# Row maxima of 32 x 512 x 1024 floats on one core: a new choice of the rows that GpSimd takes from VectorE

**Chip, cores, metric.** One core of a Trainium2 chip. The metric is the device time of one execution in microseconds (us). The span of a profile is shorter than that time, by 1.7 to 1.9 us for nearly all kernels here; two kernels that are an exception matter below.

## The reference

```python
x = np.random.randn(32, 512, 1024).astype(np.float32)   # 67.1 MB
def reference(x):
    return np.max(x, axis=-1)
```

The kernel must read all of x once. In the profile of the kernel before, the queue that does it is busy 96.7% of the span of 162.3 us, and its last piece lands at 158.98 us.

## The kernel before

The 16384 rows lie on 128 partitions. A load brings n rows to every partition ("row" is from here on a row on each of the 128 partitions, thus 128 x 1024 numbers). Loads 0 to 16 bring 15, 15, 15, 14, 12, 11, 9, 8, 7, 6, 4, 3, 2, 2, 1, 1 and 1 rows into a ring, and three pieces bring the last two rows. One queue on SyncE issues them all.

VectorE reduces rows along the free dimension. To spare it work in the late part, some 128-column parts of some late loads go another way: TensorE turns them (128 x 128 transposes into PSUM), ScalarE copies them to SBUF, GpSimd takes the maximum over the partitions, TensorE brings the one row of result back into a column, and VectorE merges. `SHARED` says which: load: (rows, parts of eight).

```python
SHARED = {7: (2, 3), 9: (4, 4), 11: (3, 3), 13: (2, 3), 16: (1, 1)}
TENSOR = [("turn", 7, 0), ("back", 7, 0), ("turn", 9, 0), ...]   # order on TensorE
MERGE = {8: (7,), 12: (9,), 15: (11,), 18: (13, 16)}             # behind which load to merge
...
    # turn(j, c): q rows by `parts` transposes, then
    in_turn("ACT", nc.scalar.copy(out=sb[:, :W], in_=ps[:, :W]))
    in_turn("POOL", nc.gpsimd.partition_all_reduce(
        top[:, :W], sb[:, :W], P, bass_isa.ReduceOp.max))
...
    # for each load j on VectorE:
        if n > m:
            maximum(res[:, col:col + n - m], rows(j)[:, :n - m, :])        # whole rows
        if m and parts < C:
            maximum(share(j)[:, parts, :], rows(j)[:, n - m:, parts * P:]) # the rest of shared rows
        merge(j)
...
    # the end: three pieces with the last two rows
    latest_row = maximum(res[:, AT - 1:AT], piece)          # piece 1: 689 columns
    merge(len(loads))
    maximum(<two results>, <piece 2 and what piece 1 gave>) # the pair, 2 x 336 columns
    merge(len(loads) + 1)
    maximum(res[:, I - 1:I], res[:, MID - 1:])              # piece 3: 689 columns
    # stores: three behind latest_row, the last behind everything
```

A row that is shared with all eight parts needs no partial reduction on VectorE; a row with three parts needs one of 640 columns.

## Time and profile before

| | before |
|---|---|
| median time | 164.06 us (163.99 to 164.13, 6 runs) |
| span of the profile | 162.3 us |
| DMA queue of the loads | 96.7% of the span |
| VectorE (DVE) busy | 135.4 us, 83% |
| GpSimd busy | 16.2 us |

The chain of work that ended last, by engine, and the group of GpSimd's all-reduces (busy us, mean ns of one, and idle time before them):

```profile
DVE 57%; DMA 36%; issue 5%; DVEq 0%
...
L143 POOL PARTITION_ALL_REDUCE top<-sb x7 | 16.0, 2330 | 141.8 <-ACT sb L141 141.8
```

The chain names VectorE as the main limit.

### The profile page before, as it was taken

What the parts mean: (1) busy time and instruction counts of PE and PEld (TensorE: products, weight loads), DVE (VectorE), ACT (ScalarE), POOL (GpSimd) and SP (SyncE); (2) the same over time, 40 slices, a digit from 0 to 9 for tenths busy, and PEclk for the clock granted to TensorE, in tenths of its full rate; (3) what the DMA queues carried; (4) which work ended last, traced back from release to release, by engine and by line L of the source; (5) the groups of instructions that cost most, each with busy time, mean ns of one, the idle gap of its engine ahead of it and who ended that gap; (6) DMA issues with size and microseconds to landing.
All of it is one profiled execution on the core that took longest, in us unless ns stands there. A gap on an engine that the chain in (4) does not pass through costs nothing.

```text
span 162.3 us, 305 instructions
## 1 busy us (share of the span) xinstructions
PE 14.0 (9%) x76; PEld 12.0 (7%) x76; DVE 135.4 (83%) x35; ACT 6.3 (4%) x8; POOL 16.2 (10%) x11
## 2 busy tenths in 40 slices
PE   0000000000000000000000000000003010736540
PEld 0000000000000000000000000000002010725440
DVE  3000079995999779998999999999999999999994
ACT  3000000000000000000000000000001000222020
POOL 0000000000000000000000000000000500095970
DMA  7999699988999699999998998999999999999990
GB/s 242 485 485 454 273 485 485 485 379 348 485 485 485 285 410 452 452 452 388 497 472 371 433 455 355 436 436 420 509 396 445 452 395 396 440 411 423 405 379 18
DMA packets 3200, 67.18 MB, mean 414 GB/s; under 512 B 640, under 2 KB 640, under 8 KB 1408
## 3 DMA queue, kind: packets, MB, share of 16 engines
q1 hardware_dynamic: 2880, 67.11, 96.7%
q10 hardware_dynamic: 320, 0.07, 0.2%
HBM read 67.11 MB, written 0.07 MB: 414 GB/s over the span
## 4 chain that ended last, share of the span: by engine, by line
DVE 57%; DMA 36%; issue 5%; DVEq 0%
DVE res L168 52%; DMA ring<-in_x_dram 36%; DVE fetched L168 5%; DVEq L249 0%
## 5 line engine op out<-in xcount | busy, mean ns | idle before, releaser
L168 DVE TENSOR_REDUCE res<-ring 128x15 f32<-128x15360 f32 (+10 forms) x15 | 124.1, 8302 | 23.7 <-DMA ring<-in_x_dram 23.7
L143 POOL PARTITION_ALL_REDUCE top<-sb x7 | 16.0, 2330 | 141.8 <-ACT sb L141 141.8
L135 PE MATMUL ps<-ident,ring 128*128 128x128 f32 x38 | 9.3, 425 | 133.8 <-DMA ring<-in_x_dram 133.8
L135 PEld LDWEIGHTS ps<-ident,ring 128*128 128x128 f32 x38 | 7.5, 223 | 134.1 <-issue 127.8
L141 ACT COPY sb<-ps 128x768 f32<-128x768 f32 (+3 forms) x7 | 5.1, 739 | 150.2 <-PE ps L135 150.2
L168 DVE TENSOR_REDUCE fetched<-ring 128x2 f32<-128x1280 f32 (+3 forms) x5 | 8.5, 1699 | 0.0
L161 PE MATMUL fetched<-ident,top 1*128 1x1 f32 x38 | 4.8, 243 | 10.8 <-DVE fetched L168 7.3
L161 PEld LDWEIGHTS fetched<-ident,top 1*128 1x128 f32 x38 | 4.5, 213 | 12.5 <-issue 8.0
L168 DVE TENSOR_REDUCE res<-res 128x2 f32<-128x672 f32 (+1 forms) x2 | 1.7, 858 | 0.0
L141 ACT ACT_TABLE_LOAD x1 | 1.3, 1283 | 0.7 <-PEq L238 0.7
L83 DVE MEMSET ident<- 128x128 f32 x1 | 0.2, 165 | 0.8 <-PEq L238 0.8
L168 DVE TENSOR_REDUCE res<-fetched 128x2 f32<-128x8 f32 (+3 forms) x5 | 0.7, 158 | 0.0
L90 DVE TENSOR_SCALAR rowno<-rowno 32x1 f32<-32x1 f32 x3 | 0.4, 146 | 0.1
L85 DVE TENSOR_TENSOR_SCAN colno<-ident 128x128 f32<-128x128 f32 x1 | 0.4, 425 | 0.0
L92 DVE TENSOR_SCALAR ident<-colno,rowno 128x128 f32<-128x128 f32 x1 | 0.3, 285 | 0.0
L87 DVE STREAM_TRANSPOSE rowno<-colno 128x32 f32<-128x32 f32 x1 | 0.2, 213 | 0.0
L238 POOL MEMSET const-float32-0.0<- 128x1 f32 x1 | 0.1, 98 | 0.2 <-issue 0.2
L238 POOL MEMSET const-bfloat16-1.0<- 128x1 bf16 x1 | 0.1, 101 | 0.0
L238 POOL MEMSET const-uint8-127<- 128x1 uint8 x1 | 0.1, 101 | 0.0
L238 POOL MEMSET const-float32-1.0<- 128x1 f32 x1 | 0.1, 99 | 0.0
L84 DVE MEMSET rowno<- 128x32 f32 x1 | 0.1, 85 | 0.0
## 6 DMA issues: line engine op xcount, KB each, us to landing
ring<-in_x_dram SPq DMA_DIRECT2D x3, 7680.0 KB, 38.4
ring<-in_x_dram SPq DMA_DIRECT2D x1, 7168.0 KB, 37.0
ring<-in_x_dram SPq DMA_DIRECT2D x1, 6144.0 KB, 33.4
ring<-in_x_dram SPq DMA_DIRECT2D x1, 5632.0 KB, 28.6
ring<-in_x_dram SPq DMA_DIRECT2D x1, 4608.0 KB, 39.1
ring<-in_x_dram SPq DMA_DIRECT2D x1, 4096.0 KB, 33.3
ring<-in_x_dram SPq DMA_DIRECT2D x1, 3584.0 KB, 29.0
ring<-in_x_dram SPq DMA_DIRECT2D x1, 3072.0 KB, 35.9
```

The source lines that it names most:

```text
L83: in_turn("DVE", nc.vector.memset(ident, 1.0))
L84: in_turn("DVE", nc.vector.memset(rowno, 0.0))
L85: in_turn("DVE", nc.vector.tensor_tensor_scan(out=colno, data0=ident, data1=ident, initial=-1.0, op0=ALU.add, op1=ALU.mult))
L87: in_turn("DVE", nc.vector.transpose(out=rowno, in_=colno[:, :32]))
L90: in_turn("DVE", nc.vector.tensor_scalar(out=part, in0=part, scalar1=float(q * 32), scalar2=None, op0=ALU.add))
L92: in_turn("DVE", nc.vector.tensor_scalar(out=ident, in0=colno, scalar1=rowno[:, 0:1], scalar2=None, op0=ALU.is_equal))
L135: in_turn("PE", nc.tensor.transpose(out=ps[:, k * P:(k + 1) * P], in_=rows(j)[:, loads[j][1] - m + r + i, c0 * P:(c0 + 1) * P], identity=i ...
L141: in_turn("ACT", nc.scalar.copy(out=sb[:, :W], in_=ps[:, :W]))
L143: in_turn("POOL", nc.gpsimd.partition_all_reduce(top[:, :W], sb[:, :W], P, bass_isa.ReduceOp.max))
L161: in_turn("PE", nc.tensor.transpose(out=share(j)[:, c0, r + i:r + i + 1], in_=tops[j, c][0:1, k * P:(k + 1) * P], identity=ident[0:1, 0:1],))
L168: return in_turn("DVE", nc.vector.reduce_max(out=out, in_=in_, axis=X))
L238: nc = _bacc.Bacc("TRN2", target_bir_lowering=False, num_devices=1)
```

## The change

The intent: give GpSimd a different set of parts. One full row each of loads 8, 10 and 11 (all eight parts, so no partial reduction is left for VectorE), and three parts of three rows of load 9 and of two rows of load 13. Loads 7 and 16 are no longer shared. 38 parts become 39, seven all-reduces become six. The load sizes do not change. Line numbers in the changed kernel are one lower.

```diff
-SHARED = {7: (2, 3), 9: (4, 4), 11: (3, 3), 13: (2, 3), 16: (1, 1)}
+SHARED = {8: (1, 8), 9: (3, 3), 10: (1, 8), 11: (1, 8), 13: (2, 3)}
 TENSOR = [
-    ("turn", 7, 0), ("back", 7, 0), ("turn", 9, 0), ("turn", 9, 1),
-    ("back", 9, 0), ("turn", 11, 0), ("turn", 11, 1), ("back", 9, 1),
-    ("turn", 13, 0), ("back", 11, 0), ("back", 11, 1), ("turn", 16, 0),
-    ("back", 13, 0), ("back", 16, 0),
+    ("turn", 8, 0), ("back", 8, 0), ("turn", 9, 0), ("turn", 9, 1),
+    ("turn", 10, 0), ("back", 9, 0), ("back", 9, 1), ("turn", 11, 0),
+    ("back", 10, 0), ("turn", 13, 0), ("back", 11, 0), ("back", 13, 0),
 ]
-MERGE = {8: (7,), 12: (9,), 15: (11,), 18: (13, 16)}
+MERGE = {9: (8,), 10: (9,), 12: (10,), 15: (11,), 18: (13,)}
```

## The prediction

> **What bounds the kernel now.** I read the page first: busy shares, groups, chain. Here is its page, in pieces.
>
> ```profile
> span 162.3 us, 305 instructions
> ...
> PE 14.0 (9%) x76; PEld 12.0 (7%) x76; DVE 135.4 (83%) x35; ACT 6.3 (4%) x8; POOL 16.2 (10%) x11
> ...
> q1 hardware_dynamic: 2880, 67.11, 96.7%
> ...
> L168 DVE TENSOR_REDUCE res<-ring 128x15 f32<-128x15360 f32 (+10 forms) x15 | 124.1, 8302 | 23.7 <-DMA ring<-in_x_dram 23.7
> L168 DVE TENSOR_REDUCE fetched<-ring 128x2 f32<-128x1280 f32 (+3 forms) x5 | 8.5, 1699 | 0.0
> ```
>
> Two things are nearly full: the 16 DMA engines (96.7%) and VectorE (DVE), whose only real idle time is 23.7 us, all spent waiting for a load. The early timeline puts that idle time before 74.64 us (18.91 + 1.98 + 1.99 + 0.79 us before the first four loads, 0 to 3), so DVE works without a visible gap from 74.64 us to its last reduction. That looks DVE-bound, in which case every column taken off DVE would pay. So the next question is how late the loads land. A landing is the issue time from the timeline of the load queue plus the time to landing from the DMA issues in the same narrow window; for loads 10, 12 and 16 and for the last piece:
>
> ```profile
> 103.47 0.42 SPq L185 DMA_DIRECT2D ring<-in_x_dram  x1
> ring<-in_x_dram SPq DMA_DIRECT2D x1, 2048.0 KB, 40.3
> 114.78 0.43 SPq L185 DMA_DIRECT2D ring<-in_x_dram  x1
> ring<-in_x_dram SPq DMA_DIRECT2D x1, 1024.0 KB, 35.2
> 131.63 0.33 SPq L185 DMA_DIRECT2D ring<-in_x_dram  x1
> ring<-in_x_dram SPq DMA_DIRECT2D x1, 512.0 KB, 24.7
> 147.52 0.33 SPq L207 DMA_DIRECT2D res<-in_x_dram  x1
> res<-in_x_dram SPq DMA_DIRECT2D x1, 344.0 KB, 11.5
> ```
>
> That gives 143.8, 150.0, 156.3 and 159.0 us. In the same way, from the records themselves to a hundredth: load 7 lands at 123.10, 8 at 131.62, 9 at 138.92, 10 at 143.81, 11 at 147.50, 12 at 149.98, 13 at 152.47, 14 at 153.76, 15 at 155.04, 16 at 156.31, the three pieces at 157.22, 158.13 and 158.98. DVE's timeline of the last stretch:
>
> ```profile
> 143.83 4.42 DVE L168 TENSOR_REDUCE res<-ring 128x4 f32<-128x4096 f32 x1
> ...
> 155.06 1.22 DVE L168 TENSOR_REDUCE res<-ring 128x1 f32<-128x1024 f32 x1
> ...
> 156.34 1.09 DVE L168 TENSOR_REDUCE fetched<-ring 128x1 f32<-128x896 f32 x1
> ...
> 157.34 0.86 DVE L168 TENSOR_REDUCE res<-ring 128x1 f32<-128x689 f32 x1
> ...
> 158.24 0.85 DVE L168 TENSOR_REDUCE res<-res 128x2 f32<-128x672 f32 x1
> 159.01 0.22 DVE L168 TENSOR_REDUCE res<-fetched 128x2 f32<-128x8 f32 x2
> 159.15 0.86 DVE L168 TENSOR_REDUCE res<-res 128x1 f32<-128x689 f32 x1
> ```
>
> DVE starts each load's work within a few hundredths to some tenths of its landing: load 10 after 0.02 us, 15 after 0.02, 16 after 0.03, the last piece after 0.17. So DVE's continuity hides a tie: from about 140 us on, DVE and the loads arrive together, and whatever DVE saves early it spends waiting. Only what DVE does after 156.31 us can move the end.
>
> [...] 15 rows take 16154 ns and one row 1214 ns, thus 1067 ns a row and 147 ns fixed, of which some 85 ns lie under the next instruction (starts 143.83 and 148.17 are 4.34 us apart, the duration is 4.42). [...] 2048 columns took 2.27 us (from 139.41) beside a GpSimd that was idle, and 2.28 us (from 141.60 and from 150.23) beside its all-reduce. [...] the windows show 442 GB/s at 20 to 40 us and 414 to 428 between 139 and 151 us. [...]
>
> **The change part by part.** A "part" is 128 columns of a row. Taken from DVE before: 2x3 + 4x4 + 3x3 + 2x3 + 1 = 38 parts; after: 8 + 3x3 + 8 + 8 + 2x3 = 39. One part is 1067 / 8 = 133 ns of DVE.
>
> *Instructions on DVE.* Of the reductions of rows straight into the result, loads 11 and 16 get one each again (13 alone has none): 15 become 17. Of the partial reductions into fetched, only those of loads 9 and 13 stay: 5 become 2. The merges stay five. So DVE has one instruction less, some 60 ns of unhidden fixed cost, and 133 ns less work: in all about 0.2 us less busy time of 135.4.
>
> *Loads.* The sizes do not change. Every slot that a late load reuses belonged to loads 0 to 5, and the last issues waited for landings eight loads before (131.63, 138.93, 143.82 and 147.52 us follow the landings of loads 8 to 11). Nothing that the change moves releases a load; the landings should stay where they are.
>
> *DVE replayed against the landings*, with durations from the groups by shape and about 0.085 us overlap: load 7 starts at 123.96 as now, eight whole rows give 8.59, so load 8 starts at 132.55 (0.74 later than now). Its six rows: 6.46, to 139.01. Load 9: three rows 3.26, partial 2.06, merge 0.08: to 144.41, where now load 10 starts at 143.83. Load 10 with three rows instead of four: 3.26, merge 0.08: 147.75 (now 148.17). Load 11 with two rows: 2.19: 149.94. Load 12 has landed only at 149.98, so it starts at 150.0, 2.19 and a merge 0.09: 152.28, where load 13 has landed only at 152.47. So the 0.25 us by which DVE now comes to load 12 after its landing is gone, and what DVE saved is spent in two waits (about 0.05 and 0.2 us). From load 13 on the sequence is as now: 152.49, 153.88, 155.06, 156.20 for the merge of load 11.
>
> *The end.* Load 16 starts at 156.34 as now, but reads 1024 columns in place of 896: 1.21 us in place of 1.09, +0.12. Its own merge (start to start 0.07) is gone, with the transpose, copy and all-reduce of that row. The last reduction thus starts at 159.15 + 0.12 - 0.07 = 159.20, and the last store goes out 0.05 us later. Sum: +0.05 us on 164.05.
>
> *GpSimd's chain.* All-reduces by width: 1024 columns 3.2 us, 768 2.5, 384 1.5. After: 1024, 768, 384, 1024, 1024, 768, together 16.1, in place of the 16.0 busy us of seven calls. Load 8: lands 131.62, transposes 1.9, copy 1.0, all-reduce 3.2: to 138.0, eight transposes back by 139.1, needed at 144.3. Load 9: all-reduces end at 144.0 and 145.5; its transposes back stand behind load 10's turn on TensorE (to 145.8) and are done by about 147.0, needed at 147.67. Load 10: copy done 146.9, all-reduce to 150.2, back by 151.3, needed at 152.2. Load 11: all-reduce 150.7 to 153.9, back by about 155.0, needed at 156.2. Load 13: 155.0 to 157.5, back by 158.3, needed at 159.1. Each has at least 0.6 us to spare by this estimate.
>
> **The rivals.** *A, DVE-bound:* the lack of idle time before every late reduction speaks for it. Then the 0.2 us saved would arrive at the end: 163.85. Against it stand the landings: the last piece lands at 158.98 and its reduction already starts at 159.15, so no more than 0.17 can come off, and in the replay DVE meets landings at load 12 to 16 first. *B, the merge of load 9 or 11 is late:* GpSimd now hands back three whole rows, and load 9's merge comes one load after its own instead of three. If its transposes back ended 1 us later than I place them, DVE would stand 0.3 to 0.5 us there; load 12's wait of 0.05 and load 13's of 0.2 would swallow half: 164.2 to 164.4. It needs an all-reduce that takes longer than its width says; the two 1024-column ones took 3.22 and 3.30, so I give it little. *C, the landings move* because fewer or other readers touch the ring: [...] a shift of a few tenths either way remains. *D, a whole-row share is cheap enough to be a real gain over 2%,* 3.3 us: DMA busy 96.7% of the span leaves no room.
>
> **Range and chances.** My path gives 164.1, A 163.85, B up to 164.4; the spread of the runs before is 0.08 us. So the predicted time is 164.1 us, the range 163.8 to 164.4. A 2% difference needs 3.3 us, which none of these reaches: faster 0.01, same 0.98, slower 0.01.
>
> **What would show it.** In the changed profile: landings within 0.1 us of those above; DVE busy about 135.2 us; gaps before the reductions of loads 12 and 13 of 0.05 and 0.2 us, in which the releaser is a load; six all-reduces in place of seven; load 8's work starting near 132.55, load 16's at 156.34 with 1.21 us, the last reduction near 159.2. I am wrong if DVE waits for TensorE or fetched before a merge (rival B), if load 16's work starts earlier than 156.3 us (the landings moved), or if the last reduction starts before 159.1 us with the landings in place (rival A).

The forecast's sum is +0.12 - 0.07 = +0.05 us on 164.05 us.

## The result and the profile after

The changed kernel took 164.18 us in the median (164.00 to 164.21, 6 runs) against 164.06 us: ratio 1.0006, 95% interval 0.9993 to 1.0019. It is the same at 2%, and inside the predicted range. Ratios here are the mean time of one kernel's fast runs over the mean of the other's of the same rounds, so they are not quite the ratios of the medians.

The page of the changed kernel, with the lines that answer to those above:

```profile
span 162.4 us, 298 instructions
...
PE 14.2 (9%) x78; PEld 12.1 (7%) x78; DVE 135.3 (83%) x34; ACT 6.3 (4%) x7; POOL 16.3 (10%) x10
...
q1 hardware_dynamic: 2880, 67.11, 96.6%
...
DMA 58%; DVE 39%; SPq 0%; issue 0%; DVEq 0%
...
L167 DVE TENSOR_REDUCE res<-ring 128x15 f32<-128x15360 f32 (+10 forms) x17 | 128.4, 7593 | 23.7 <-DMA ring<-in_x_dram 23.7
L142 POOL PARTITION_ALL_REDUCE top<-sb x6 | 16.1, 2697 | 141.1 <-ACT sb L140 141.1
...
L167 DVE TENSOR_REDUCE fetched<-ring 128x3 f32<-128x1920 f32 (+1 forms) x2 | 3.6, 1824 | 0.2 <-DMA ring<-in_x_dram 0.2
```

The counts are those of the diff: 17 reductions from the ring straight into the result (the first piece's among them), 2 partial ones, 6 all-reduces. The chain has turned from "DVE 57%, DMA 36%" to "DMA 58%, DVE 39%", though neither the loads nor VectorE's total work has changed by more than some tenths of a us. The reason is the last line: VectorE now idles visibly for 0.2 us before a partial reduction, waiting for a load, and a chain that is followed back from the end switches to DMA at that gap. Before, VectorE met the loads with no gap, so the chain stayed on VectorE. Here VectorE and the loads run level, and a gap of 0.2 us was enough to turn the shares.

VectorE's timeline of the last stretch in the changed kernel (start, duration, both in us):

```profile
150.00 2.29 DVE L167 TENSOR_REDUCE res<-ring 128x2 f32<-128x2048 f32 x1
152.20 0.16 DVE L167 TENSOR_REDUCE res<-fetched 128x1 f32<-128x8 f32 x1
152.56 1.50 DVE L167 TENSOR_REDUCE fetched<-ring 128x2 f32<-128x1280 f32 x1 [0.20 <-DMA ring<-in_x_dram]
...
156.34 1.22 DVE L167 TENSOR_REDUCE res<-ring 128x1 f32<-128x1024 f32 x1
...
158.37 0.85 DVE L167 TENSOR_REDUCE res<-res 128x2 f32<-128x672 f32 x1
159.14 0.16 DVE L167 TENSOR_REDUCE res<-fetched 128x2 f32<-128x8 f32 x1
159.26 0.87 DVE L167 TENSOR_REDUCE res<-res 128x1 f32<-128x689 f32 x1
```

The landings of loads 7 to 16 and of the pieces differ from those before by at most 0.02 us (load 16: 156.31 in both; last piece: 158.98 in both). VectorE arrives early at load 12 and load 13 and waits; load 16's work starts at 156.34 as before; from there on the path is 0.11 us longer (the last reduction starts at 159.26 in place of 159.15).

### The profile page after: what moved, and what is told of

The parts are those of the page before. It is cut to its first block, busy times and chain, and to the rows that moved or that the text cites. A ratio compares the mean times of both kernels' runs of the same rounds, so it can differ in the third digit from the quotient of the medians.

```text
span 162.4 us, 298 instructions
## 1 busy us (share of the span) xinstructions
PE 14.2 (9%) x78; PEld 12.1 (7%) x78; DVE 135.3 (83%) x34; ACT 6.3 (4%) x7; POOL 16.3 (10%) x10
## 4 chain that ended last, share of the span: by engine, by line
DMA 58%; DVE 39%; SPq 0%; issue 0%; DVEq 0%
DMA ring<-in_x_dram 58%; DVE res L167 38%; DVE fetched L167 1%; SPq L184 0%; DVEq L167 0%
## 5 line engine op out<-in xcount | busy, mean ns | idle before, releaser
L167 DVE TENSOR_REDUCE res<-ring 128x15 f32<-128x15360 f32 (+10 forms) x17 | 128.4, 7593 | 23.7 <-DMA ring<-in_x_dram 23.7
L140 ACT COPY sb<-ps 128x1024 f32<-128x1024 f32 (+2 forms) x6 | 5.0, 852 | 148.0 <-PE ps L134 148.0
L167 DVE TENSOR_REDUCE fetched<-ring 128x3 f32<-128x1920 f32 (+1 forms) x2 | 3.6, 1824 | 0.2 <-DMA ring<-in_x_dram 0.2
L167 DVE TENSOR_REDUCE res<-fetched 128x1 f32<-128x8 f32 (+2 forms) x5 | 0.8, 157 | 0.0
```

What stands on the lines that cost most here:

```text
L167: return in_turn("DVE", nc.vector.reduce_max(out=out, in_=in_, axis=X))
```

## The experiments

Theory: **the landing of load 16 and VectorE's work after it set the end; work saved before it turns into waiting.** Rival A: VectorE is the bound from 74.64 us on and each column counts. Rival B: a merge waits for GpSimd's way. Rival C: landings depend on VectorE or on who reads the ring.

A yardstick is needed, since single runs of one kernel differ by some tenths of a us (the changed kernel by 0.6 us in its second set). The records of the profiled executions show one cause: the first load lands somewhat earlier or later (21.23 to 21.53 us), and all later landings move along with it; from load 0's landing to load 16's it took 134.90 to 134.97 us in every profile. So I compare the time from load 16's landing to the start of the last reduction, the **tail**, as well as mean times.

| run | load 16 lands | last reduction starts | tail | mean time, and of the kernel before in the same rounds |
|---|---|---|---|---|
| kernel before | 156.31 | 159.15 | 2.84 | |
| changed kernel | 156.31 | 159.26 | 2.95 | 164.16, 164.06 |
| changed, again | 156.17 | 159.12 | 2.95 | 164.26, 164.03 |
| load 16 shared again | 156.28 | 159.18 | 2.90 | 164.14, 164.03 |
| before, load 16 whole | 156.33 | 159.27 | 2.94 | 164.19, 164.03 |
| load 16: two parts shared | 156.38 | 159.33 | 2.95 | 164.32, 164.03 |
| load 11's merge late | 156.15 | 159.12 | 2.97 | 164.15, 164.08 |
| half the columns | 156.24 | 159.18 | 2.94 | 164.22, 163.97 |
| load 8 cut | 156.35 | 159.29 | 2.94 | 164.18, 164.02 |
| dummy behind load 12 | 156.34 | 159.28 | 2.94 | 164.26, 164.08 |
| dummy behind load 16 | 156.31 | 159.45 | 3.14 | 164.35, 164.08 |
| load 9 back late | 156.31 | 161.77 | 5.46 | 166.68, 163.97 |
| second row of load 8 | 156.46 | 159.40 | 2.94 | 164.87, 164.08 |
| 16 idle transposes | 156.36 | 159.31 | 2.95 | 164.91, 164.02 |

Landings and the last starts are from each trace's records. A tail comes from one profile, and of the kernel before only one is kept; but eight of the profiles (the changed kernel twice and six of its or the old kernel's variants) have the same work on VectorE behind load 16, and their tails agree within 0.01 us. In time, every run is "the same" as the kernel before at 2%. The 95% interval of the ratio lies wholly above 1 only for "two parts shared", "dummy behind load 16", "load 9 back late" and the last two rows; differences of 0.1 us between the others are told by the tail, not by the time.

### 1. The changed kernel again

> The changed kernel once more, as the base for the runs beside it. My theory (the landing of load 16 at 156.31 us and what VectorE does after it set the end): last reduction starts at 159.26 us as before in its profile, time some 0.1 us over the kernel before, 164.15 to 164.2. Rival A (VectorE is the bound from 74.64 us on, every column counts): 0.2 us under the kernel before.

Tail 2.95 us again; ratio 1.0013 (interval 1.0000 to 1.0026). The changed kernel is if anything slower by 0.1 to 0.2 us, not faster by 0.2 as rival A has it.

### 2. Does VectorE's earlier work matter at all? Half the columns of loads 0 to 12

```diff
-            maximum(res[:, col:col + n - m], rows(j)[:, :n - m, :])
+            maximum(res[:, col:col + n - m], rows(j)[:, :n - m, :H if j <= 12 else D])
```

> The changed kernel with VectorE reading half the columns of the whole rows of loads 0 to 12 (a wrong result on purpose): about 59 us less work on VectorE. My theory: the landings stay within 0.1 us, since the load queue never runs dry, and the end stays within 0.05 us of the changed kernel. Rival A: tens of us faster. Rival C (landings depend on when slots come free or on who reads): landings earlier than 156.2 us for load 16.

VectorE's groups (busy, mean ns, idle before):

```profile
L167 DVE TENSOR_REDUCE res<-ring 128x15 f32<-128x7680 f32 (+10 forms) x17 | 67.7, 3989 | 81.6 <-DMA ring<-in_x_dram 81.6
```

Its timeline at the end:

```profile
156.26 2.00 DVE L167 TENSOR_REDUCE res<-ring 128x1 f32<-128x1024 f32 x2
...
159.18 0.87 DVE L167 TENSOR_REDUCE res<-res 128x1 f32<-128x689 f32 x1
```

VectorE's busy time fell from 135.3 to 74.9 us, and its waits for loads rose from 23.7 to 81.6 us. The time did not fall: 164.22 us in the mean, tail 2.94. Rival A is refuted as plainly as can be, and so is C: ring slots came free up to 8 us earlier and loads 3 to 14 were issued 2.4 to 8.1 us earlier, yet load 16 landed within the usual scatter (134.90 us after load 0). The loads kept their pace: 427, 425 and 411 GB/s at 0 to 74, 74 to 140 and 140 to 156 us, against 426, 426 and 412 in the changed kernel. That the load queue never runs dry, as the expectation has it, the records of the changed kernel show: each load was issued at least 10.6 us before the one ahead of it landed. In this run VectorE also waits 1.6 us in all for merges (releaser: TensorE), and these waits cost nothing either, since later waits for loads swallow them.

### 3. The same relief as one row, without more instructions

```diff
-            maximum(res[:, col:col + n - m], rows(j)[:, :n - m, :])
+            maximum(res[:, col:col + n - m], rows(j)[:, :n - m, :853 if j == 8 else D])
```

> The changed kernel with load 8's direct reduction cut to 853 of 1024 columns (a wrong result on purpose): one row's worth, 1.07 us, less work for VectorE at the place of the earlier relief of load 8, but with no instruction more on any engine. My theory: VectorE waits for load 9 (138.9 us) instead, the last reduction still starts 2.95 us after the landing of load 16, and the time is that of the changed kernel (within 0.1 us), with the usual 1.8 us between span and time. Rival A: 1.07 us faster. If the time is 0.3 us or more over the changed kernel, as in the run that gave GpSimd a second row, the relief itself costs something that I do not see.

```profile
139.00 3.36 DVE L167 TENSOR_REDUCE res<-ring 128x3 f32<-128x3072 f32 x1 [0.92 <-DMA ring<-in_x_dram]
```

This line is load 9's first reduction in this run: VectorE waits 0.92 us for load 9 and is then where it was. Tail 2.94, time as the changed kernel. What is saved at load 8 is spent at load 9.

### 4. The same added work at two places

A dummy reduction of 128 columns, behind load 12's or behind load 16's (`junk` is a tile of its own):

```diff
             maximum(res[:, col:col + n - m], rows(j)[:, :n - m, :])
+        if j == 12:      # in the other run: 16
+            maximum(junk[:, 0:1], rows(j)[:, 0, :P])
```

> The changed kernel with a dummy reduction of 128 columns after load 12's (about 0.2 us from start to start). My theory: it falls into the gap of 0.2 us in which VectorE waits for load 13, so the end moves by 0 to 0.05 us. Rival A: +0.2 us.

> The same dummy reduction after load 16's. My theory: all of it is on the path, +0.2 us over the changed kernel (164.35 to 164.4), the last reduction starts at 159.45 us. Rival A: +0.2 us too, the same as at load 12; so it's the difference between the two places that tells.

Behind load 12 the partial reductions (load 13's is one of the two) show no idle time any more, and the last reduction starts as it does in the changed kernel's profile, within 0.03 us:

```profile
L169 DVE TENSOR_REDUCE fetched<-ring 128x3 f32<-128x1920 f32 (+1 forms) x2 | 3.6, 1824 | 0.0
...
159.28 0.87 DVE L169 TENSOR_REDUCE res<-res 128x1 f32<-128x689 f32 x1
```

Behind load 16 the timeline shows the dummy and what it moved:

```profile
156.34 1.22 DVE L169 TENSOR_REDUCE res<-ring 128x1 f32<-128x1024 f32 x1
157.47 0.27 DVE L169 TENSOR_REDUCE junk<-ring 128x1 f32<-128x128 f32 x1
...
159.45 0.87 DVE L169 TENSOR_REDUCE res<-res 128x1 f32<-128x689 f32 x1
```

Tail 3.14 us there, which is 0.19 more; behind load 12 it is 2.94 us, and the idle 0.2 us before load 13's reduction is gone from the waits. The same instruction costs nothing before load 16's landing and all of its 0.2 us after it. In mean time the two differ by 0.09 us only (164.26 and 164.35, ranges 164.10 to 164.39 and 164.27 to 164.39), which the start's scatter covers; here the tail is the better witness.

### 5. Is load 16 the whole of the loss?

First the kernel before with load 16 whole, then the changed kernel with load 16 shared as before:

```diff
-SHARED = {7: (2, 3), 9: (4, 4), 11: (3, 3), 13: (2, 3), 16: (1, 1)}
+SHARED = {7: (2, 3), 9: (4, 4), 11: (3, 3), 13: (2, 3)}
```

```diff
-SHARED = {8: (1, 8), 9: (3, 3), 10: (1, 8), 11: (1, 8), 13: (2, 3)}
+SHARED = {8: (1, 8), 9: (3, 3), 10: (1, 8), 11: (1, 8), 13: (2, 3), 16: (1, 1)}
```

(with the entries of load 16 in TENSOR and MERGE taken out and put in)

> The kernel before, with only load 16's share taken back by VectorE (896 columns become 1024, its merge goes). My theory: this one part makes the whole of the change's result, so the last reduction starts at 159.26 us and the time is 0.1 us over the kernel before, as that of the changed kernel. Rival A: +0.12 - 0.07 = +0.05 us. If the loss comes from another part of the change, this run equals the kernel before.

> The changed kernel, but load 16 shares its 128 columns with GpSimd as in the kernel before. My theory: load 16's reduction starts at 156.34 us still and takes 1.09 in place of 1.21 us, so the last reduction starts 0.11 us earlier, 159.15 us; time as the kernel before within 0.05 us. Rival A: VectorE has then 0.3 us less work than in the kernel before, so 163.75. Rival B (a merge that waits for GpSimd): with an all-reduce more at the end, no gain or a loss.

The first gives the changed kernel's tail, 2.94 us:

```profile
156.35 2.00 DVE L168 TENSOR_REDUCE res<-ring 128x1 f32<-128x1024 f32 x2
...
159.27 0.87 DVE L168 TENSOR_REDUCE res<-res 128x1 f32<-128x689 f32 x1
```

Of all the parts of the change, this one alone makes the difference in the tail. The second was expected to give 2.84 and gave 2.90:

```profile
156.37 1.09 DVE L168 TENSOR_REDUCE fetched<-ring 128x1 f32<-128x896 f32 x1
...
159.18 0.86 DVE L168 TENSOR_REDUCE res<-res 128x1 f32<-128x689 f32 x1
```

The reduction takes its 1.09 us, but it starts 0.09 us after the landing (156.28), where in the kernel before it was 0.02 (156.313 to 156.337). In the records a separate wait for the load stands in front of it here, and it waits for one of VectorE's own earlier results too; in the kernel before the same reduction carries the load's wait alone. So more than half of what sharing load 16 is worth was lost ahead of this start. That the second wait took it is my estimate from the records. The merge just ahead ends 0.03 us before this start and so could be the cause too; but load 13's reduction, which has the same two waits, starts 0.09 us after its landing in the changed kernel although the merge ahead of it ended 0.20 us before (landing 152.46, the wait's own record at 152.49, start 152.56). No run takes the second wait away.

### 6. What is a merge at the end worth?

```diff
-MERGE = {9: (8,), 10: (9,), 12: (10,), 15: (11,), 18: (13,)}
+MERGE = {9: (8,), 10: (9,), 12: (10,), 18: (13, 11)}
```

> The changed kernel with load 11's merge moved from behind load 15 to the end, beside load 13's. The prediction took 0.07 us for a merge at the end. In the profiles the last reduction starts 0.03 us after the end of the one over the two halves, with one merge or two between. If that is what sets it, the second merge costs 0.02 us at most: last reduction at 159.28 us. If a merge there costs its own 0.07: 159.33 us. At its old place the merge lies before load 16's landing, so taking it away there gives nothing.

```profile
158.20 0.85 DVE L167 TENSOR_REDUCE res<-res 128x2 f32<-128x672 f32 x1
158.97 0.23 DVE L167 TENSOR_REDUCE res<-fetched 128x2 f32<-128x8 f32 x2
159.12 0.86 DVE L167 TENSOR_REDUCE res<-res 128x1 f32<-128x689 f32 x1
```

Two merges lie between the pair's reduction and the last one, and the tail is 2.97, 0.02 more than with one. The records say why: the last reduction takes up a number that the pair's wrote, so it waits for the pair's end. Without any merge it could not start much before 159.09 here (158.20 + 0.85 is 159.05, and 0.03 us or so passes). One merge fits into that wait; the second sticks out by 0.02 us, not by the 0.07 us from its start to the next. (The number without any merge is reckoned, since no run leaves both out; with one merge, the last reduction starts 0.03 us after the pair's end in all ten profiles that have one merge there. With two it is not 0.03 us, as the expectation has it, but 0.05 in the kernel before: 159.09 to 159.15.)

### 7. Can a late merge hold the end? Load 9 brought back behind load 11's turn

```diff
-    ("turn", 10, 0), ("back", 9, 0), ("back", 9, 1), ("turn", 11, 0),
+    ("turn", 10, 0), ("turn", 11, 0), ("back", 9, 0), ("back", 9, 1),
```

> The changed kernel with TensorE's turn of load 11 put ahead of the transposes that bring load 9 back, so that those end near 150.6 us, 2.9 us after VectorE wants them at 147.65 us. If a late merge holds VectorE and everything behind it, the wait at load 13 (0.3 us) swallows some and the end moves by about 2.6 us: 166.8 us. It shows what rival B would have looked like in a profile. If the end moves much less, there was slack that I don't see.

```profile
144.39 3.34 DVE L167 TENSOR_REDUCE res<-ring 128x3 f32<-128x3072 f32 x1
150.60 0.17 DVE L167 TENSOR_REDUCE res<-fetched 128x3 f32<-128x12 f32 x1 [2.87 <-PE fetched L160]
```

This is rival B: a merge with 2.87 us of idle time in front, released by TensorE, and an end that is 2.5 us later. The changed kernel's waits hold no line of the kind "DVE <- PE fetched", so B is real but not at work there.

### 8. A version that should have won: two parts of load 16 shared

```diff
-SHARED = {8: (1, 8), 9: (3, 3), 10: (1, 8), 11: (1, 8), 13: (2, 3)}
+SHARED = {8: (1, 8), 9: (3, 3), 10: (1, 8), 11: (1, 8), 13: (2, 3), 16: (1, 2)}
```

(with the same entries in TENSOR and MERGE as in experiment 5)

> The changed kernel with 256 columns of load 16 shared with GpSimd. My theory: load 16's reduction takes 0.96 us from 156.34 us, the pieces' reductions then start with their landings (157.22, 158.12 us) and the last one at 159.05 us, 0.2 us earlier than in the changed kernel: time 163.95 to 164.0, 0.1 us under the kernel before. Nothing more can come, since the last piece lands at 158.98 us. Rival B: its all-reduce (1.1 us by its width, behind load 13's that ends at 157.6 us) comes back after 159.1 us and the last reduction waits: 159.2 us or later.

```profile
156.47 0.96 DVE L168 TENSOR_REDUCE fetched<-ring 128x1 f32<-128x768 f32 x1
...
158.84 0.37 PE L161 MATMUL fetched<-ident,top 1*128 1x1 f32 x2 [0.33 <-POOL top L143]
159.04 0.37 DVE L168 TENSOR_REDUCE res<-fetched 128x2 f32<-128x8 f32 x2
159.33 0.87 DVE L168 TENSOR_REDUCE res<-res 128x1 f32<-128x689 f32 x1
```

My theory's number was 159.05 and failed; the rival in the expectation was right. VectorE had its columns off, but load 16's way over GpSimd, behind load 13's all-reduce, came back only at 159.21 (158.84 + 0.37). Its merge started at 159.25, and the last reduction behind it. With the time 0.29 us over the kernel before, none of these runs beats the kernel before.

### 9. A second row of load 8 to GpSimd, and where its time went

```diff
-SHARED = {8: (1, 8), 9: (3, 3), ...
+SHARED = {8: (2, 8), 9: (3, 3), ...
```

(and one turn and one back more in TENSOR)

> The changed kernel with a second whole row of load 8 given to GpSimd: VectorE does 1.07 us less. My theory: load 9 has landed only at 138.91 us, so VectorE waits there for about 1 us, meets load 12 and 13 as before, and the end doesn't move (within 0.05 us of the changed kernel). Rival A: 1.07 us faster than the changed kernel, 163.1 us.

The tail is 2.94 and the spans average 162.45 us against 162.30 of the kernel before, just as the theory says. But the time is 164.87 in the mean, 0.8 over the kernel before: between span and time lie 2.0 to 2.1 us in four runs and 3.1 to 3.2 in two, where all other kernels have 1.7 to 1.9. The loss is outside the profiled span. This run has 94 matmuls where the changed kernel has 78. So I put 16 idle transposes into the changed kernel, at its beginning, where TensorE has nothing else to do (in the changed kernel its first matmul starts at 131.70 us):

```diff
+    ps = psum.tile([P, D], F32)
+    for k in range(16):
+        in_turn("PE", nc.tensor.transpose(
+            out=ps[:, k % C * P:(k % C + 1) * P], in_=ident, identity=ident))
```

> The changed kernel with 16 more transposes on TensorE in its idle beginning (of the identity, into a PSUM buffer that is overwritten), so with as many TensorE instructions as the run that gave GpSimd a second row of load 8. In that run the span was that of the changed kernel, but the time lay 2.0 to 3.2 us over the span, in place of 1.8. If the number of TensorE instructions does it, this run shows 2.0 us or more between span and time; if not, 1.8 us, and the cause stays open. The span itself should not move (within 0.1 us of the changed kernel).

```profile
L96 PE MATMUL ps<-ident 128*128 128x128 f32 x16 | 3.7, 425 | 2.6 <-DVE ident L91 2.6
```

These 3.7 us of work between 2.6 and some 6 us delay nothing: tail 2.95. Yet 2.0 to 2.1 us lie between span and time in four runs, 2.8 and 3.35 in two, as in the run above. So these 16 matmuls, with their weight loads, cost 0.2 to 1.5 us outside the span; a run with 82 matmuls (experiment 8) still had 1.8. The two programs are also the longest of all (335 and 331 instructions, the others at most 313), so it is not shown whether TensorE's count or the total matters. The four executions with 2.8 us or more all list a clock below 1 (0.93 and 0.53), but two others at those clocks had 2.0 to 2.1, and the kernel before has 1.7 to 1.8 at 0.95. What happens there, the profile does not show, and it stays open.

## Why the prediction was right

That the time fell into the range proves little: rival A's 163.85 and rival B's 164.4 lie in it too, and a difference of 2% was out of reach for all of them. What was right is the mechanism, and that is read from starts, landings and tails.

**The replay against the landings held.** "Load 8 starts at 132.55": 132.54. "Load 10 at 144.41": 144.39. "Load 11 at 147.75": 147.73. "Load 12 at 150.0": 150.00. "Load 13 at 152.49": 152.56, 0.09 us after the landing; a separate wait for the load stands in front, as in experiment 5. Of the two gaps that it named as a sign, the profile shows the one of 0.2 us before load 13; the 0.05 us before load 12 do not show as idle time (the last paragraph of this part says why). "Load 16 at 156.34": 156.34.

**What VectorE saved early was spent waiting,** as the replay said; experiments 2, 3 and 4 show it with savings of 60 us, 1.07 us and an addition of 0.2 us. Rival A is out.

**The landings stayed** (rival C), even with VectorE half idle, and **the merges were in time** (rival B); experiment 7 shows what it costs when they are not. The all-reduces ended within 0.15 us of the predicted times: load 9's second at 145.37, predicted 145.5; load 10's at 150.30, predicted 150.2; load 13's at 157.59, predicted 157.5.

**The sum's sign was right, its size not quite.** "+0.12 - 0.07 = +0.05" measured +0.13 - 0.02 = +0.11 us in the two profiles. The term that was mis-sized is the merge that goes away: I took its start-to-start time, 0.07 us. Experiment 6 shows that the last reduction waits for the pair's end anyhow, so a second merge there is worth 0.02 us. In time, the two comparisons give 0.10 and 0.23 us in the means; the scatter of the start does not let me tell these from 0.11.

**One step in it is not shown.** The prediction went from the load rates of some windows (442 GB/s at 20 to 40 us, 414 to 428 between 139 and 151 us; the DMA share of the first window reads 1.02, so they are good to about 2%) to a ceiling. No run shows a ceiling. That relief of VectorE does not hasten the loads is shown by experiment 2: with 60 us less work on VectorE the load rates stayed within 1 GB/s and the time was 164.22 us, so the 3.3 us of rival D were not there either.

**VectorE's busy time** was to fall by 0.2 us and fell by 0.1. Part of what I counted as saved is now overlap lost at a wait: load 12's reduction starts 0.08 us later after its predecessor than an unheld one would, and that time counts as busy.

## What to carry to other kernels

In the kernel before, VectorE worked from 74.64 us to its last reduction without idle time in the profile's groups, in the changed kernel with 0.2 us of it, and yet it was not the bound: 60 us less work on it left the changed kernel's time at 164.22 us (experiment 2). So put the landing of each late load beside the start of the work that needs it, and find the last point at which the two meet. In this kernel, only work behind that point moved the end (0.19 us for the dummy behind load 16, nothing for the one behind load 12), or a delay ahead of it that was longer than the waits in between (2.87 us in experiment 7, for an end 2.5 us later). Look there and not in the totals. And compare spans as well as times when an edit adds many instructions: the 16 transposes of experiment 9 added 0.2 to 1.5 us that no profile line shows.

## Figures from these profiles

- An all-reduce over the partitions took 3.22 to 3.30 us for 128 x 1024 floats, 2.50 us for 768 columns and 1.50 us for 384 (the kernel before and the changed kernel).
- In the changed kernel a reduction that does not wait starts 0.08 to 0.09 us before the end of the one ahead of it, and the last reduction, which waits for the pair's result, 0.03 us after that end (159.224 to 159.258). Where a wait for a load stands in a record of its own in front of the reduction (load 13 in the changed kernel), the start came 0.09 us after the landing; where the reduction carries that wait alone (load 16 in the kernel before), 0.02 us after it.
